# Rotary turn of queries and keys: the projection split in two parts from PSUM, each permuted by a product of its own

## Chip, cores and metric

The kernel runs on one core of a Trainium2 chip. The core has five engines with an instruction queue each: TensorE (PE), VectorE (DVE), ScalarE (ACT), GpSimd (POOL) and SyncE (SP), from whose queue the DMAs named here are issued. The metric is the device time in microseconds of one execution; smaller is better.

## What is computed

The reference is a two-layer trunk over 1024 latent tokens with a prefix of 256 context tokens, width 1024, in fp32. In each layer one input projection feeds three token mixers (windowed grouped-query attention, an SSD scan and a gated DeltaNet scan), whose outputs are joined and go through one output projection; a squared-ReLU MLP follows. Cut to what matters here, a two-dimensional rotary turn of the latent queries and keys ahead of the attention:

```python
def rot(u, pos):                      # u: 32 of the 64 columns of a head
    ang = pos[:, None] * inv_freq[None, :]
    u1, u2 = jnp.split(u, 2, axis=-1)
    return jnp.concatenate([u1 * cos - u2 * sin, u2 * cos + u1 * sin], axis=-1)

def window_gqa_attention(q_c, k_c, v_c, q_l, k_l, v_l, sink, need_ctx):
    q_l = rope_2d(q_l)                # rows turn the first half of a head, columns the second
    k_l = rope_2d(k_l)
    ...
```

Context tokens aren't turned.

## The kernel before

**Layout.** Activations lie with features on partitions and tokens on the free axis. The 1280 tokens (context first) are three chunks, `CHUNKS`: 256, 512 and 512 tokens; the first is the context. A block of 128 projected features is the product of eight 128x128 weight tiles with one chunk, accumulated in a PSUM bank `ps`. Precision is bought by splitting: every operand is a sum of a rounded fp32r part and its rest (`wh`, `wl` of weights, L192 and L193; `hl` of activations), and `proj` (L204) makes three products of each pair of tiles, 24 per block and chunk.

**The turn.** `rest()` (from L518) handles the blocks that aren't needed first; blocks 16 and 17 are the four query heads, 18 the two key heads (`j` = 0, 1, 2). Each of the three has two latent chunks, so there are 6 turns in a layer and 12 in the kernel. `perm` is a signed 128x128 permutation that brings u2 to u1's place with its sign and the reverse. For a latent chunk: SP loads the chunk of the table `rope` (cosines and sines, 512 KB) into a tile of tag `sil`, which has two buffers (L550); ACT copies `ps` to `rx` (L552); TensorE multiplies it with `perm` in fp32 into `rt` (L554); DVE makes `ry` = `rt` x sine (L556); POOL makes `rx` x cosine (L557) and adds `ry` (L558). The sum is split once more into `athl`: ACT casts (L560), DVE takes the rest (L561). `athl` is another tile of tag `sil`. From it SP stores four pieces for queries (L572) or six for keys (L567, L568) to scratch in DRAM (`attq`, `attk`), from where the attention loads them later. A context chunk skips the turn and is only split and stored. `rx` and `ry` share the two buffers of tag `st` with the copies of `to_tm` (L431).

**What sets the order.** The program is written as generators that are interleaved: while the last blocks of the projection run, the DeltaNet's inversion (`gQ`, `gT` products, DVE transposes L730, L735) and the first steps of its scan run too. A scan step has four groups of 12 small products, `vps`, `tps`, `sps` and `ops` (L837, L845, L856, L865), each waiting for a copy or a difference made from the one before; its inputs `stp`, `sv`, `sW` come by SP. Once the projection is done, attention (`asc`, `apT`, `aop`), SSD (from `sseg`, L891) and the rest of the scan run interleaved; each unit of the scan ends in `finish`: a norm (`osq`, `oss`, L800), a transposition `on` (L805), the gate `oz` (L806) and a store. The out-projection (`pu`, L204 again) follows. Within these bounds the compiler orders every engine's instructions by the program's priorities and a time line of its own, so an edit at one place may change the order of others further down.

Of the kernel before, what the change touches and what calls it, by code (L numbers as in the profile page):

```python
# [141 lines left out]
def kernel(ctx: ExitStack, tc: tile.TileContext, a: dict, out: bass.AP, dbg=None):  # L142
# [15 lines left out]
    with tc.tile_pool(name="cs0", bufs=1) as c0:  # L158
        cs2 = c0.tile([128, len(CN) - NF, 128], F32, name="cs2")
        nc.sync.dma_start(out=cs2, in_=csrc[:, NF:])  # L160
        for i, n in enumerate(CN[NF:]):
            d_, dt_ = (CR, F32R) if i < 3 else (CB, BF16)
            d_[n] = cp.tile([128, 128], dt_, name="c" + n)
            V.tensor_copy(out=d_[n], in_=cs2[:, i])
    pair = CR["pair"].bitcast(F32)
# [213 lines left out]
    def in_proj(l, hl, prm, R, es):  # L379
# [44 lines left out]
        def to_tm(s, dst, more=None):  # L424
            for u0 in (0, 4, 8):
# [4 lines left out]
                st = ip.tile([128, 4, 128], F32, tag="st", name="st")  # L430
# [87 lines left out]
        def rest():  # L518
# [24 lines left out]
            to_tm(s, lambda u0, n: R["attv"][:, u0:u0 + n])  # L543
            for j in range(3):
                for t0, n, ps in block(16 + j, ctxs=j == 2 or not last):
                    if t0 < LC:
                        x = ps[:, :n]
                    else:
                        rope = ip.tile([128, 2, 512], F32, tag="sil", name="rope", bufs=2)
                        nc.sync.dma_start(out=rope, in_=a["rope"][:, :, t0 - LC:t0 - LC + n])  # L550
                        x = ip.tile([128, 512], F32, tag="st", name="rx")
                        S.copy(out=x, in_=ps)  # L552
                        rt = Q["p"].tile([128, 512], F32, tag="pq", name="rt")
                        P.matmul(out=rt, lhsT=C["perm"], rhs=x, start=True, stop=True)  # L554
                        y = ip.tile([128, 512], F32, tag="st", name="ry")
                        V.tensor_tensor(out=y, in0=rt, in1=rope[:, 1], op=MULT)  # L556
                        G.tensor_tensor(out=x, in0=x, in1=rope[:, 0], op=MULT)  # L557
                        G.tensor_tensor(out=x, in0=x, in1=y, op=ADD)  # L558
                    t = ip.tile([128, 2, 512], F32R, tag="sil", name="athl", bufs=2)
                    S.copy(out=t[:, 0, :n], in_=x)  # L560
                    V.tensor_tensor(out=t[:, 1, :n], in0=x, in1=t[:, 0, :n].bitcast(F32), op=SUB)  # L561
                    t = t.bitcast(F32)
                    for g in range(2):
                        gs = slice(64 * g, 64 * g + 64)
                        if j == 2:
                            for g2 in range(2):
# [1202 lines left out]
```

## Time and profile before

| | us |
|---|---|
| time, median of 3 runs | 3470.7 (3467.23 to 3475.13) |
| the profiled execution, its own time | 3474.11 |
| span of that execution in the trace | 3472.3 |
| TensorE busy in it | 3169.3 |
| VectorE busy | 2367.8 |
| ScalarE busy | 1795.9 |
| GpSimd busy | 926.2 |
| mean granted TensorE clock | 0.956 of 2.4 GHz |

The span runs from the first to the last instruction. An engine's busy time leaves out its waits and its issue of DMAs; records of matmuls overlap at their ends, so the time of one product is better read from the distance between starts. In a timeline row the number in square brackets is the engine's idle time ahead of the row and what ended it. An fp32 product has two records in the trace, a product of fp32r or bf16 one; a group of 12 scan products, which are fp32, has 24.

### The profile page before, as it was taken

Reading aid. Unit: us, or ns where it says so; the run is one execution under the profiler, and the core shown is the slowest. Engines: PE = TensorE matmul, PEld = TensorE weight load, DVE = VectorE, ACT = ScalarE, POOL = GpSimd, SP = SyncE. Lnnn points to the kernel's source line nnn. Section 1 sums busy time; section 2 is a strip of 40 time slices with the busy share of each in tenths; the row PEclk is TensorE's granted clock in tenths of the full one; section 3 lists DMA queues with packets and bytes.
Section 4 is the critical chain, followed back from the end, with each engine's and each line's share of the span. In section 5 each row is a group of like instructions: output and inputs, shape, how many; then the busy total and the mean of one; then the engine's idle time right before and its main releaser. Section 6 shows DMA issues by size and latency. Waiting matters only on the chain. (4 is left out here: it accounts for less than half of the span.)

```text
span 3472.3 us, 56181 instructions
## 1 busy us (share of the span) xinstructions
PE 3169.3 (91%) x20912; PEld 2510.2 (72%) x20912; DVE 2367.8 (68%) x3725; ACT 1795.9 (52%) x3197; POOL 926.2 (27%) x822
## 2 busy tenths in 40 slices
PE   4998898899998999999989898798899998999998
PEld 1766787766676688788879666676677776887886
DVE  6568972178578556777785646986288487667776
ACT  4665533365556456444465556552366565555443
POOL 3228423477131000000120434723475120000001
PEclk8999899899999999999999999998899999999999
DMA  5467437765455754544445564745864455645442
GB/s 194 139 197 204 133 103 208 236 194 153 147 200 183 282 181 168 172 146 146 140 150 178 191 187 116 193 125 143 267 205 141 168 188 210 207 151 185 158 156 105
DMA packets 386743, 603.25 MB, mean 174 GB/s; under 512 B 64566, under 2 KB 195494, under 8 KB 382374
## 3 DMA queue, kind: packets, MB, share of 16 engines
q1 hardware_dynamic: 383590, 585.51, 53.0%
q0 software_dynamic: 2880, 14.16, 1.3%
q8 instruction: 164, 2.69, 0.3%
q14 instruction: 109, 0.89, 0.1%
HBM read 430.09 MB, written 169.46 MB: 173 GB/s over the span
## 5 line engine op out<-in xcount | busy, mean ns | idle before, releaser
L1414 PE MATMUL pu<-x,wh 128*128 128x512 f32 x3072 | 958.9, 395 | 32.4 <-ACT wh L192 14.8
L1414 PEld LDWEIGHTS pu<-x,wh 128*128 128x128 f32 x3072 | 581.0, 190 | 168.0 <-ACT wh L192 20.3
L204 PE MATMUL ps<-x,wh 128*128 128x512 f32 (+1 forms) x2288 | 681.5, 382 | 7.3 <-ACT ub L405 6.4
L1414 PE MATMUL pu<-x,wl 128*128 128x512 f32 x1536 | 597.5, 393 | 3.2 <-DVE wl L193 3.2
L204 PEld LDWEIGHTS ps<-x,wh 128*128 128x128 f32 x2288 | 420.5, 196 | 99.5 <-issue 21.6
L299 POOL TENSOR_TENSOR nacc<-nacc,nsq 128x512 f32<-128x512 f32 (+1 forms) x60 | 86.3, 1439 | 1520.8 <-ACT nsq L298 1323.4
L204 PE MATMUL ps<-x,wl 128*128 128x512 f32 (+1 forms) x1144 | 428.4, 377 | 3.5 <-POOL wl L193 3.5
L192 ACT CAST wh<-raw 128x512 fp32r<-128x512 f32 (+1 forms) x328 | 200.8, 615 | 275.3 <-PE ps L204 82.7
L1414 PEld LDWEIGHTS pu<-x,wl 128*128 128x128 f32 x1536 | 291.0, 189 | 67.2 <-DVE wl L193 5.7
L420 DVE SCALAR_TENSOR_TENSOR sil<-ub,cw,sil 128x256 f32<-128x256 f32 (+1 forms) x236 | 273.5, 1179 | 50.2 <-ACT sil L418 44.2
L204 PE MATMUL pu<-x,wh 128*128 128x256 f32 (+1 forms) x1152 | 284.7, 339 | 17.2 <-ACT x L1350 13.5
L193 POOL TENSOR_TENSOR wl<-raw,wh 128x512 fp32r<-128x512 f32 (+1 forms) x120 | 175.6, 1465 | 416.8 <-ACT wh L192 380.5
L193 DVE TENSOR_TENSOR wl<-raw,wh 128x512 fp32r<-128x512 f32 x208 | 156.1, 758 | 150.8 <-ACT wh L192 144.0
L204 PEld LDWEIGHTS ps<-x,wl 128*128 128x128 f32 x1144 | 222.6, 195 | 46.7 <-issue 7.0
L204 PEld LDWEIGHTS pu<-x,wh 128*128 128x128 f32 x1152 | 200.4, 195 | 44.1 <-issue 10.5
L204 PE MATMUL pu<-x,wl 128*128 128x256 f32 (+1 forms) x576 | 194.5, 339 | 14.1 <-DVE wl L193 14.0
L192 ACT CAST wh<-A 128x512 fp32r<-128x512 f32 x192 | 118.7, 619 | 139.5 <-PE pu L1414 133.7
L193 DVE TENSOR_TENSOR wl<-A,wh 128x512 fp32r<-128x512 f32 x192 | 135.7, 708 | 70.4 <-ACT wh L192 70.3
L1414 PE MATMUL pu<-xb,wh 128*128 128x512 f32 x512 | 163.9, 401 | 4.6 <-ACT h L1464 4.5
L1604 ACT CAST x<-x 128x1024 fp32r<-128x1024 f32 x112 | 111.9, 1048 | 103.8 <-DMA x<-th 97.9
L1662 DVE TENSOR_TENSOR xb<-pu,xb 128x512 f32<-128x512 f32 x192 | 131.1, 684 | 46.2 <-PE pu L1414 46.2
L192 ACT CAST wh<-S 128x512 fp32r<-128x512 f32 x128 | 79.0, 620 | 145.4 <-PE pu L1414 116.7
(354 smaller groups left out, 6133.1 us busy)
## 6 DMA issues: line engine op xcount, KB each, us to landing
x<-th SPq DMA_DIRECT2D x56, 1024.0 KB, 5.4
aw<-in_wada_dram SPq DMA_DIRECT2D x96, 512.0 KB, 5.7
A<-in_w_dram SPq DMA_DIRECT2D x164, 256.0 KB, 3.1
raw<-in_w_dram SPq DMA_DIRECT2D x128, 256.0 KB, 2.9
th<-h SPq DMA_DIRECT2D x128, 256.0 KB, 2.6
raw<-in_winf_dram SPq DMA_DIRECT2D x116, 256.0 KB, 3.5
stp<-rt SPq DMA_DIRECT2D x36, 768.0 KB, 5.3
xb<-in_w_dram SPq DMA_DIRECT2D x24, 1024.0 KB, 4.9
```

The source lines that it names most:

```text
L192: S.copy(out=wh[:, :n], in_=raw)
L193: eng.tensor_tensor(out=wl[:, :n], in0=raw, in1=wh[:, :n].bitcast(F32), op=SUB)
L204: P.matmul(out=ps[:, :n], lhsT=w_[:, k], rhs=x_[4 * g + k][:, :n], start=(g + k + j == 0), stop=(g == 1 and k == 3 and j == 2))
L299: eng.tensor_tensor(out=acc[:, :n], in0=acc[:, :n], in1=sq[:, :n], op=ADD)
L420: V.scalar_tensor_tensor(out=acc, in0=u[:, o + k:o + k + n], scalar=w[:, bi, k:k + 1], in1=acc, op0=MULT, op1=ADD)
L1414: P.matmul(out=ps, lhsT=w_[:, j], rhs=x_, start=first and j + i == 0, stop=(j == 3 and i == 2), skip_group_check=True)
L1604: S.copy(out=hi, in_=raw)
L1662: V.tensor_tensor(out=y[:, m], in0=ps, in1=y[:, m], op=ADD)
```

## The change

For a latent chunk ACT now casts `ps` to the rounded part `rxh`, and DVE takes the rest `rxl` = `ps` - `rxh`, both in fp32r; TensorE permutes each with `permr`, a rounded copy of `perm` made once, and sums the two products in `rt`. DVE multiplies `ps` with the cosines inside the table's tile, then `rt` with the sines in the tile's other half, and adds both there. The split of the sum (`put_att`) overwrites the same tile, and the stores read it. So a turn has one tile of tag `sil` in place of two; tag `st` has three buffers. GpSimd has no part in it. The second half of a turn (`rotate`) is written behind the next chunk's first half. Context chunks are split into a tile `athl` of their own as before.

```diff
+    permr = cp.tile([128, 128], F32R, name="permr")
+    V.tensor_copy(out=permr, in_=C["perm"])
...
-                st = ip.tile([128, 4, 128], F32, tag="st", name="st")
+                st = ip.tile([128, 4, 128], F32, tag="st", name="st", bufs=3)
...
+            def put_att(j, t0, n, x, t):
+                S.copy(out=t[:, 0, :n].bitcast(F32R), in_=x)
+                V.tensor_tensor(out=t[:, 1, :n], in0=x, in1=t[:, 0, :n], op=SUB)
...
+            def rotate(j, t0, n, rope, parts_):
+                rt = Q["p"].tile([128, 512], F32, tag="pq", name="rt")
+                for i, x in enumerate(parts_):
+                    P.matmul(out=rt, lhsT=permr, rhs=x, start=i == 0, stop=i == 1)
+                V.tensor_tensor(out=rope[:, 1], in0=rt, in1=rope[:, 1], op=MULT)
+                V.tensor_tensor(out=rope[:, 1], in0=rope[:, 0], in1=rope[:, 1], op=ADD)
+                put_att(j, t0, n, rope[:, 1], rope)
+
             for j in range(3):
+                turned = []
                 for t0, n, ps in block(16 + j, ctxs=j == 2 or not last):
                     if t0 < LC:
-                        x = ps[:, :n]
-                    else:
-                        rope = ip.tile([128, 2, 512], F32, tag="sil", name="rope", bufs=2)
-                        nc.sync.dma_start(out=rope, in_=a["rope"][:, :, t0 - LC:t0 - LC + n])
-                        x = ip.tile([128, 512], F32, tag="st", name="rx")
-                        S.copy(out=x, in_=ps)
-                        rt = Q["p"].tile([128, 512], F32, tag="pq", name="rt")
-                        P.matmul(out=rt, lhsT=C["perm"], rhs=x, start=True, stop=True)
-                        y = ip.tile([128, 512], F32, tag="st", name="ry")
-                        V.tensor_tensor(out=y, in0=rt, in1=rope[:, 1], op=MULT)
-                        G.tensor_tensor(out=x, in0=x, in1=rope[:, 0], op=MULT)
-                        G.tensor_tensor(out=x, in0=x, in1=y, op=ADD)
-                    t = ip.tile([128, 2, 512], F32R, tag="sil", name="athl", bufs=2)
-                    S.copy(out=t[:, 0, :n], in_=x)
-                    V.tensor_tensor(out=t[:, 1, :n], in0=x, in1=t[:, 0, :n].bitcast(F32), op=SUB)
...
+                        put_att(j, t0, n, ps[:, :n], ip.tile([128, 2, 512], F32, tag="sil", name="athl", bufs=2))
+                        continue
+                    rope = ip.tile([128, 2, 512], F32, tag="sil", name="rope", bufs=2)
+                    nc.sync.dma_start(out=rope, in_=a["rope"][:, :, t0 - LC:t0 - LC + n])
+                    xh = ip.tile([128, 512], F32R, tag="st", name="rxh", bufs=3)
+                    S.copy(out=xh, in_=ps)
+                    V.tensor_tensor(out=rope[:, 0], in0=ps, in1=rope[:, 0], op=MULT)
+                    if turned:
+                        rotate(*turned.pop())
+                    xl = ip.tile([128, 512], F32R, tag="st", name="rxl", bufs=3)
+                    V.tensor_tensor(out=xl, in0=ps, in1=xh.bitcast(F32), op=SUB)
+                    turned.append((j, t0, n, rope, (xh, xl)))
+                rotate(*turned.pop())
```

The line numbers of the new kernel are two larger up to `to_tm` and 14 larger behind the turn (L837 is L851 there). The instructions are the same on every engine up to the first `rt`, but for the copy to `permr`; behind it the order differs in the rest of the mixers of layer 0 and, from the input projection on, of layer 1. Three places follow.

VectorE, layer 0, the first two turns, before (`vd` belongs to the scan):

```order
L839 TENSOR_TENSOR vd<-vps,sv 128x384
L556 TENSOR_TENSOR ry<-rt,rope 128x512
L561 TENSOR_TENSOR athl<-rx,athl 128x512
L839 TENSOR_TENSOR vd<-vps,sv 128x384
L556 TENSOR_TENSOR ry<-rt,rope 128x512
L839 TENSOR_TENSOR vd<-vps,sv 128x384
L561 TENSOR_TENSOR athl<-rx,athl 128x512
```

The same place with the change:

```order
L853 TENSOR_TENSOR vd<-vps,sv 128x384 x2
L581 TENSOR_TENSOR rope<-ps,rope 128x512
L585 TENSOR_TENSOR rxl<-ps,rxh 128x512
L567 TENSOR_TENSOR rope<-rt,rope 128x512
L568 TENSOR_TENSOR rope<-rope 128x512
L581 TENSOR_TENSOR rope<-ps,rope 128x512
L585 TENSOR_TENSOR rxl<-ps,rxh 128x512
L549 TENSOR_TENSOR rope<-rope 128x512
L567 TENSOR_TENSOR rope<-rt,rope 128x512
```

The product of `ps` with the table (L581) stands ahead of the rest `rxl` (L585), which the second `rt` product reads; the first turn's split (L549) now stands behind the second turn's L581 and L585.

TensorE, layer 0, around the first `rt`, before (`ps` are products of the projection):

```order
L204 MATMUL ps<-x_437,wh 128x256
L204 MATMUL ps<-x_438,wh 128x256
L554 MATMUL rt<-rx,cst 128x512
L204 MATMUL ps<-x_437,wl 128x256
L204 MATMUL ps<-x,wh 128x512 x2
L204 MATMUL ps<-x,wl 128x512
```

The second product of the first turn, with the change (the first one stands 65 rows ahead; `vps`, `tps` belong to the scan):

```order
L851 MATMUL vps<-X_5717,stp 64x64
L859 MATMUL tps<-vd,stp 64x64 x12
L566 MATMUL rt<-rxl,permr 128x512
L206 MATMUL ps<-x,wh 128x512 x2
L206 MATMUL ps<-x,wl 128x512
```

Before, the product stood among the projection's products of one chunk, and the next chunk's came right behind; now six groups of the scan stand between the first and the second product, and the next chunk's products stand behind the second.

TensorE, the end of layer 1's mixers, before (`on` belongs to the scan's `finish`, `pu` to the out-projection):

```order
L1141 MATMUL apT<-cst,aP 128x128 x4
L805 MATMUL on<-cst,oacc 128x128 x3
L1141 MATMUL apT<-cst,aP 128x128 x4
L1147 MATMUL aop<-aPT,attv 64x256
L1141 MATMUL apT<-cst,aP 128x128 x4
L1147 MATMUL aop<-aPT,attv 64x256 x3
L1141 MATMUL apT<-cst,aP 128x128 x4
L1147 MATMUL aop<-aPT,attv 64x256 x4
L204 MATMUL pu<-x,wh 128x512 x3
```

With the change (`ops` is the last group of the scan):

```order
L879 MATMUL ops<-X_26284,stp 64x64
L1155 MATMUL apT<-cst,aP 128x128 x4
L1161 MATMUL aop<-aPT,attv 64x256 x3
L1155 MATMUL apT<-cst,aP 128x128 x4
L1161 MATMUL aop<-aPT,attv 64x256 x4
L819 MATMUL on<-cst,oacc 128x128 x6
L206 MATMUL pu<-x,wh 128x512 x3
```

The last scan group now stands ahead of the last eight `apT`, and the six `on` behind the last `aop`, right ahead of the out-projection.

## Rows read from the trace of the kernel before

**Rows 1.** The page, busy time of each engine, share of the span, instructions.

```profile
PE 3169.3 (91%) x20912; PEld 2510.2 (72%) x20912; DVE 2367.8 (68%) x3725; ACT 1795.9 (52%) x3197; POOL 926.2 (27%) x822
```

**Rows 2.** Busy us (count) by stretch: PE, PEld, DVE, ACT, POOL; granted clock, DMA share, GB/s.

```profile
528.60:660.85 132.25, 118.53 (x1218) 95.39 (x1217) 21.69 (x38) 43.47 (x88) 47.31 (x44) 0.99 0.70 212
2363.00:2481.80 118.80, 102.38 (x1131) 80.34 (x1129) 42.10 (x60) 34.95 (x63) 42.73 (x38) 0.89 0.62 183
```

**Rows 3.** TensorE's waits, 515 to 660 us: total us, times, longest.

```profile
PE rt L554 <- ACT rx L552: 10.0, 4, 4.2
```

**Rows 4.** TensorE's waits, 2365 to 2480 us.

```profile
PE rt L554 <- ACT rx L552: 9.3, 4, 5.0
```

**Rows 5.** ScalarE's timeline, layer 1: start, us, operation, idle time before, releaser.

```profile
2411.02 0.62 ACT L560 CAST athl<-rx 128x512 fp32r<-128x512 f32 x1 [8.80 <-POOL rx L558]
2411.66 0.58 ACT L552 COPY rx<-ps 128x512 f32<-128x512 f32 x1
```

**Rows 6.** TensorE's timeline, layer 1, the longest wait.

```profile
2412.30 2.07 PE L554 MATMUL rt<-rx,cst 128*128 128x512 f32 x2 [4.99 <-ACT rx L552]
2413.39 1.84 PE L204 MATMUL ps<-x,wh 128*128 128x512 f32 x2
...
2416.65 0.63 PE L204 MATMUL ps<-x,wh 128*128 128x512 f32 x2
```

**Rows 7.** VectorE's timeline, layer 0, the first table product.

```profile
550.38 0.69 DVE L556 TENSOR_TENSOR ry<-rt,rope 128x512 f32<-128x512 f32 x1 [7.55 <-DMA rope<-in_rope_dram]
```

**Rows 8.** TensorE's timeline, layer 0, around one `rt`.

```profile
546.10 0.91 PE L845 MATMUL tps<-vd,stp 64*64 64x64 f32 x24
...
554.38 1.13 PE L554 MATMUL rt<-rx,cst 128*128 128x512 f32 x2 [2.84 <-ACT rx L552]
554.94 1.03 PE L204 MATMUL ps<-x,wh 128*128 128x512 f32 x2
555.81 0.40 PE L204 MATMUL ps<-x,wl 128*128 128x512 f32 x1
556.04 0.62 PE L204 MATMUL ps<-x,wh 128*128 128x512 f32 x2
```

**Rows 9.** Views of `rope`, `rx` and `athl`: count, ns min/median/max; landing.

```profile
L556 DVE TENSOR_TENSOR ry<-rt,rope x12: 691/692/693, 550.4 to 2454.9; 128x512 f32<-128x512 f32 x12
DMA to landing us min/median/max: 3.8/4.1/4.4
...
L558 POOL TENSOR_TENSOR rx<-rx,ry x12: 1259/1264/1292, 551.8 to 2456.6; 128x512 f32<-128x512 f32 x12
L560 ACT CAST athl<-rx x12: 612/617/622, 553.1 to 2457.9; 128x512 fp32r<-128x512 f32 x12
L561 DVE TENSOR_TENSOR athl<-rx,athl x12: 691/692/1087, 553.7 to 2458.6; 128x512 fp32r<-128x512 f32 x12
...
DMA to landing us min/median/max: 2.1/3.1/6.3
```

**Rows 10.** VectorE's timeline, layer 0, one `oacc`.

```profile
591.52 1.65 DVE L800 TENSOR_TENSOR oacc<-oacc,oss 128x384 f32<-128x384 f32 x1 [0.36 <-POOL oss L799]
```

**Rows 11.** VectorE's timeline, layer 1, the inversion's transposes.

```profile
2375.78 4.06 DVE L730 STREAM_TRANSPOSE Lb<-XX 128x1024 f32<-128x1024 f32 x2
```

**Rows 12.** TensorE's timeline, the first `sseg` of either layer.

```profile
660.85 0.68 PE L891 MATMUL sseg<-ag,cst 128*128 128x60 f32 x4 [1.10 <-ACT wst L901]
...
2481.78 0.88 PE L891 MATMUL sseg<-ag,cst 128*128 128x60 f32 x6 [0.18 <-ACT zg L579]
```

**Rows 13.** Timelines of TensorE and VectorE, end of layer 1's mixers.

```profile
2685.38 0.74 PE L865 MATMUL ops<-X,stp 128*64 128x64 f32 x18
...
2696.51 0.66 PE L1141 MATMUL apT<-cst,aP 128*128 128x128 f32 x4
...
2707.39 1.65 PE L204 MATMUL pu<-x,wh 128*128 128x512 f32 x3 [6.83 <-ACT x L1350]
...
2695.15 0.62 DVE L806 SCALAR_TENSOR_TENSOR oz<-on,dg,oz 128x384 f32<-128x384 f32 x1 [0.70 <-PE on L805]
```

More of the change, by code (lines that the diff above doesn't have):

```diff
@@ L543, in rest @@
             to_tm(s, lambda u0, n: R["attv"][:, u0:u0 + n])
+            def put_att(j, t0, n, x, t):
+                S.copy(out=t[:, 0, :n].bitcast(F32R), in_=x)
+                V.tensor_tensor(out=t[:, 1, :n], in0=x, in1=t[:, 0, :n], op=SUB)
+                t = t.bitcast(F32)
+                for g in range(2):
+                    gs = slice(64 * g, 64 * g + 64)
+                    if j == 2:
+                        for g2 in range(2):
+                            nc.sync.dma_start(out=R["attk"][64 * g2:64 * g2 + 64, g, t0:t0 + n], in_=t[gs, 0, :n])
+                        nc.sync.dma_start(out=R["attk"][gs, 2, t0:t0 + n], in_=t[gs, 1, :n])
+                    else:
+                        for k in range(2):
+                            o = 64 * (g ^ k)
+                            nc.sync.dma_start(out=R["attq"][t0 // 128:(t0 + n) // 128, o:o + 64, 2 * g + j].rearrange("u p f -> p u f"),
+                                              in_=t[gs, k, :n].rearrange("p (u f) -> p u f", f=128))
@@ L559, in rest @@
-                    t = ip.tile([128, 2, 512], F32R, tag="sil", name="athl", bufs=2)
-                    S.copy(out=t[:, 0, :n], in_=x)
-                    V.tensor_tensor(out=t[:, 1, :n], in0=x, in1=t[:, 0, :n].bitcast(F32), op=SUB)
[L562 to L566, printed above, removed]
-                                nc.sync.dma_start(out=R["attk"][64 * g2:64 * g2 + 64, g, t0:t0 + n], in_=t[gs, 0, :n])
-                            nc.sync.dma_start(out=R["attk"][gs, 2, t0:t0 + n], in_=t[gs, 1, :n])
-                        else:
-                            for k in range(2):
-                                o = 64 * (g ^ k)
-                                nc.sync.dma_start(out=R["attq"][t0 // 128:(t0 + n) // 128, o:o + 64, 2 * g + j].rearrange("u p f -> p u f"),
-                                                  in_=t[gs, k, :n].rearrange("p (u f) -> p u f", f=128))
+                        put_att(j, t0, n, ps[:, :n], ip.tile([128, 2, 512], F32, tag="sil", name="athl", bufs=2))
```

## The prediction, made before the changed kernel was run

> **What bounds the kernel now.** I first read the page's line of busy times: TensorE is busy 91% of the span [rows 1], so a change of the time has to come out of TensorE's idle time, out of its products, or out of its clock. The rotation lies in two stretches, one per layer, from the last products ahead of the first `rt` to the first `sseg`, with which the attention, SSD and DeltaNet work begins. The view of busy time by stretch gives them 132.25 and 118.8 us, with TensorE busy 118.5 and 102.4 [rows 2]: 13.7 and 16.4 us are idle, and the second runs at a mean granted clock of 0.89. That is the whole store this change can draw on, beside its own products.
>
> Next the waits of TensorE in both stretches: `rt` of L554 waits for ACT's copy `rx` (L552) 10.0 us in layer 0 and 9.3 us in layer 1, four times in each [rows 3, 4]. All else there is small. Why the copy is late shows in ACT's timeline at the longest one: the cast `athl` of the chunk before stands idle 8.80 us for POOL's `rx` (L558), and the next chunk's copy runs only right behind it, at 2411.66 [rows 5]. The product follows at 2412.30, after 4.99 us of idle time [rows 6]. The pair of products behind it has a record of 1.84 us; a pair some 3 us later has 0.63 [rows 6], so the clock had dropped to the lower level, 1.2 GHz, and came back. And POOL is late because the table is late: VectorE's `ry` at 550.38 had idled 7.55 us for the `rope` load [rows 7]. So the table's arrival, then ACT's order, then TensorE.
>
> **What the change removes.** (1) Products. In the PE timeline `rt` starts at 554.38 and the `wl` product of the first triple at 555.81, with two `wh` products between; the next product starts 0.23 after that one [rows 8]. So the fp32 product takes 1.43 - 2 x 0.23 = 0.97 us. The change makes two fp32r products of it, which I price as the neighbours of the same shape and type: 0.46. That saves 0.51 x 12 = 6 us of TensorE, 3 in each layer, and all of it is on TensorE's path. The rows hold this exactly, so its bounds are narrow, 5 to 6.5.
> (2) The 10.0 + 9.3 us of waits for `rx`: POOL's two operations (some 1.26 us each [rows 9]) leave the chain, and ACT's cast of the next chunk no longer stands behind a cast that waits for POOL. Whether the time comes back depends on what is late next.
>
> **What it adds.** (3) VectorE. Two operations per chunk (L556, L561) become five of 128x512. Each is 0.69 us [rows 9], with the operand in PSUM (L556) or without (L561), so 3 x 0.69 x 12 = 25 us more on VectorE, and one copy of `perm` at the start (a 128x128 tile, far from any wait). VectorE is busy 68% [rows 1], and in these stretches 21.7 of 132 and 42.1 of 119 us [rows 2]: it has room, so I put this at 0, save where one of the five stands in a chain. The worst of the rows: `athl` once took 1.09 us against 0.69 [rows 9], so up to 60 x 0.4 = 24 us of VectorE more; it would be in idle time as well.
> VectorE's `oacc` of L800, both inputs in SBUF, took 1.65 us at 591.52 [rows 10], while POOL worked. The Trainium skill, "SBUF — State Buffer", section "Who interferes with whom", says that a VectorE instruction with two SBUF inputs and a GpSimd instruction that reads SBUF shut each other out for a whole instruction. By that rule the new sums (two SBUF inputs, one more per chunk than before) can each lose a GpSimd operation's time, and the removal of POOL's 24 operations gives back about as much; the trace agrees as far as this row goes, and the sum would be the same by either reading.
>
> (4) The wait that takes the old one's place. `rt` now needs `rxl`, and on VectorE the product with the table's cosine half, in place in the table tile, stands in the row ahead of `rxl` (it is so in the order shown). So TensorE's second product waits for the table, where before the product waited only for the copy of the chunk before. And the tile holds table, sum and result in one: the load for chunk n+2 may start only when the output DMAs of chunk n have landed. Before, the table's tile was free after VectorE and POOL had read it. The loop of one tile, from rows [rows 9]: table landing 4.1, five VectorE operations 3.5, ACT's cast 0.6, the product 0.2, four DMA issues of some 0.6 and the last one's landing 3.1: 13.9 us, for two chunks, if nothing is in the way. TensorE has 2 x 24 in-projection products of 0.23, 11 us, per such pair and several groups of the DeltaNet scan; the loop also has VectorE's, ACT's and SP's other work in it.
> I went through the new order by hand with the durations of before. Layer 0: the first table load has the same place on SP's queue, so it lands at 550.4 as before [rows 7]; cosine product and `rxl` 1.4 more, hence `rt` at 552. Between the two `rt` products stand only 14 products of half the width, 0.12 each by that, and six groups of the scan of 0.91 at most (24 records, as at 546.10 [rows 8]): some 7 us of work and the scan's own waits, from 538.4 on, where before 24 products of the next chunk stood there as well. So TensorE would idle 3.6 to 5.8 us there. The third and fifth chunk (same tile again) come at 575 and 597.5 with some 2.9 and 3.8 us; the others without. Sum 10.3 to 12.5, in place of 10.0. In layer 1 the same way: 2.1 behind the transposes of the inversion that stand on VectorE (the first pair took 4.06 us [rows 11]), 0.4, 5.9 for the fourth chunk's table, 2.5 and 1.2: 12.1 in place of 9.3; the other waits there (`gQ`, scan) become about 5.5 in place of 6.9. Bounds of this term: nothing (VectorE's order lets `rxl` pass, the waits vanish) and 19 (each as long as the longest today, 4.99, four times in either layer).
> (5) The longest waits bring half a clock with them. At the level of rows 6 this is some 1 to 2 us in layer 0 (the fifth is then shorter) and nothing sure in layer 1, where 5.9 takes the place of 4.99.
> (6) The number of DMAs stays, the same loads and 76 outputs, only issued from another tile. The third buffer of tag `st` (L431 too) I put at 0: no wait for one is among those of TensorE there [rows 3, 4]; the bound is a gain of some 1 us. What is queued behind a waiting `rope` load on SP, in program order, is weight loads (`raw`) and the loads of the scan (`sv`, `sW`, `stp`). The in-projection's weights are some chunks ahead; the scan isn't.
> (7) Order downstream. By the hand replay `sseg` of layer 0 comes some 5 to 10 us before 660.85 [rows 12], but with 30 of the scan's groups done and not 33 (2.6 us to be done later); in layer 1 some 7 to 9 us before 2481.78 [rows 12], with five groups less (4.3 us). TensorE-bound as the next stage is, that work comes back in full. So the two stretches give: layer 0, 3 + 10.0 - 11.4 + 1.5, about 3 by waits, and 2 to 7 by positions, I take 5; layer 1, 3 + 9.3 - 12.1 + 1.4, about 2 by waits and 4 by positions, I take 4. Together -9.
> (8) The end of layer 1's mixers. The last rows of TensorE before the out-projection are now the six `on` of the DeltaNet's last unit, behind the last `aop`. Before, `on` stood some 15 rows ahead. From the last `ops` product (2685.38 + 0.74) to the end of the last `oz` (2695.15 + 0.62) the chain took 9.65 us [rows 13]. In the new order the last `ops` have eight `apT` and seven `aop` behind them; that same lot ran from 2696.51 to 2700.56, where the 6.83 us of idle time ahead of 2707.39 begin [rows 13], so 4.05 us. The last `oz` would then be done 9.65 - 4.05 = 5.6 us behind the last `aop`, and the out-projection starts so much later: I take +5, bounds 0 (the first products need other units) and +6. Layer 0's end keeps its order.
>
> **The sum.** -5 - 4 + 5 = -4 us: the profiled execution's 3474.11 would become 3470. That execution lies 3.4 over the median of the runs, so 3466.7, which I give as 3466.5. What a measurement of this kernel can tell from no change is about 0.2%, 6.9 us: faster begins below 3463.8 and slower above 3477.6.
>
> **Rivals.**
> A. The waits vanish. If VectorE's cosine product is never late, or the scan fills TensorE, then -19.3 (all waits for `rx`), -6 (products) and +5 (end): -20, 3450.5. For it: VectorE has idle time, and ACT's order no longer ties chunk to chunk. Against it: the table's load was the late one already [rows 7], and its tile now comes free later. 0.2.
> B. The waits move as I said, but layer 1's end costs nothing, since the scheduler's `on` may be ready long before (the scan's chain of before had slack), or the out-projection starts with other units: -9 to -10, 3461. 0.18.
> C. Slower: the table's return loop. Outputs landed within 3.1 us at the median and 6.3 at most [rows 9]. If behind a fuller SP queue each of the six pairs waits 2 us or more beyond my replay, for a landing that is nearer 6.3 or for an issue behind scan loads, TensorE waits 12 us more: 3466.5 + 12 = 3478.5, up to +19 with the full 3.2 each. It decides from 11 / 6 = 1.9 us per pair. For it: two tiles only, and results in them; against it: SP is seldom full in these stretches, and outputs of 0.1 MB each are short. 0.22.
> D. The change doesn't do what it says: for the second and fourth chunk of layer 0 the two products stand in neighbouring rows, so nothing of the next chunk is between them and the cast; that is in my replay already and gives no time of its own.
>
> **Chances.** Forecast (within 0.2%) 0.4; A 0.2 and B 0.18, faster; C 0.22, slower. So faster 0.38, same 0.4, slower 0.22. The range reaches to A's time on the one side and past C's nearer price on the other: 3449 to 3481. The forecast's own range, by the bounds of (7) and (8), is 3460 to 3473.
>
> **What would show it right or wrong.** The `rt` products in the profile after: half the TensorE time, 0.23 each (1). POOL without rows in the rotation (2). TensorE's waits for `rxl`, some five to eight of 1 to 6 us, with VectorE idle for the `rope` load ahead of them; if TensorE's waits before `rt` sum to under 5 us, A is right, and over 30, C (4). `sseg` at 649 to 656 and at 2465 to 2475 less what layer 0 gave (7). The out-projection of layer 1 starting 10 us or more behind the last `aop` (8). Wrong altogether would be a difference that lies outside these stages, in MLP or modulation, whose order on TensorE is the same row by row.

## The result and the profile after

The changed kernel takes 3507.7 us (median of four, 3504.6 to 3511.6) beside 3469.1 us before in the same comparison: 1.0099 of the time before, interval 1.0080 to 1.0118, so about 1% slower (39 us between the medians, 34 by the ratio). A second measurement (run e13) gave 3498.0 us and 1.0090, interval 1.0074 to 1.0107. The forecast was 3466.5, and the range to 3481 doesn't hold it.

The page's line of busy times, to be held against [rows 1]:

```profile
PE 3179.2 (91%) x20912; PEld 2519.2 (72%) x20912; DVE 2409.6 (69%) x3762; ACT 1800.4 (51%) x3199; POOL 893.5 (25%) x798
```

GpSimd lost 33 us, as the removal of its operations says; VectorE gained 42; TensorE's busy time rose by 10, though its products became cheaper. Four stretches show where the 34 us between the two spans (3506.3 and 3472.3) went: in each layer from the first `rt` to the first `sseg`, which I call the rotation's stage, and from there to the first product of the out-projection, the mixers' stage. Busy time by stretch, first of the changed kernel, then of the kernel before (columns as in [rows 2]):

```profile
532.90:651.40 118.50, 104.04 (x1085) 85.64 (x1083) 29.56 (x50) 35.88 (x72) 24.89 (x25) 0.96 0.70 207
651.40:919.00 267.60, 230.88 (x2218) 163.93 (x2218) 177.26 (x406) 145.14 (x342) 158.46 (x174) 0.87 0.53 166
2391.30:2491.90 100.60, 82.82 (x949) 65.02 (x947) 45.44 (x68) 29.12 (x51) 21.38 (x20) 0.92 0.64 182
2491.90:2738.90 247.00, 211.86 (x2493) 154.45 (x2493) 165.66 (x353) 139.98 (x318) 145.77 (x162) 0.90 0.62 191
```

```profile
538.40:658.60 120.20, 107.58 (x1156) 85.84 (x1154) 19.30 (x32) 38.55 (x77) 42.17 (x39) 0.99 0.69 210
658.60:904.40 245.80, 218.54 (x2146) 157.38 (x2146) 167.50 (x406) 142.44 (x336) 159.07 (x172) 0.91 0.57 177
2375.80:2481.80 106.00, 89.58 (x1070) 69.81 (x1068) 30.06 (x38) 31.77 (x57) 39.76 (x36) 0.87 0.66 193
2481.80:2707.40 225.60, 201.25 (x2374) 145.52 (x2374) 157.09 (x352) 136.67 (x312) 141.32 (x158) 0.95 0.63 192
```

The rotation's stages are 1.7 and 5.4 us shorter; ahead of the first `rt` another 5.5 us went. The mixers' stages are 21.8 and 21.4 us longer. What lies between and behind them changed by 0.9 and 2.5. So -5.5 - 1.7 + 21.8 + 0.9 - 5.4 + 21.4 + 2.5 = 34.0: the loss lies wholly behind the rotation, in work that the change doesn't touch.

Two cautions. The 5.5 us aren't a gain of the change: the instructions there are the same but for the copy to `permr`, and runs e10 and e12, whose order is the same up to there, reach their first `rt` at 538.2 and 530.1. So one trace of each kernel splits the loss no finer than some 8 us a stretch. And the rotation's stages hold less work: by TensorE's counts three and five scan groups (72 and 119 records) have moved from them into the mixers' stages. By the prediction's estimate these are 2.6 and 4.3 us, about the 7.1 us by which the rotation's stages are shorter, so the rotation itself shows no gain here.

In the rotation's stages the waits ahead of `rt`, to be held against [rows 3, 4], are now of VectorE's `rxl`, in the changed kernel's list of TensorE's waits (us, times, longest; layer 0, then layer 1):

```profile
PE rt L566 <- DVE rxl L585: 11.9, 3, 5.2
...
PE rt L566 <- DVE rxl L585: 9.1, 4, 3.3
PE rt L566 <- DVE rope L567: 1.2, 1, 1.2
```

Layer 0's 11.9 us are in place of 10.0, layer 1's 10.3 in place of 9.3. The first of them, on VectorE and TensorE:

```profile
545.44 0.69 DVE L581 TENSOR_TENSOR rope<-ps,rope 128x512 f32<-128x512 f32 x1 [3.78 <-DMA rope<-in_rope_dram]
546.04 0.68 DVE L585 TENSOR_TENSOR rxl<-ps,rxh 128x512 fp32r<-128x512 f32 x1
...
546.78 0.79 PE L566 MATMUL rt<-rxl,permr 128*128 128x512 f32 x1 [4.16 <-DVE rxl L585]
```

VectorE stood idle for the table; the cosine product L581 went first, `rxl` (L585) behind it, and TensorE had waited 4.16 us for that. A product of either part passes in 0.23 us where the clock is full, as here in layer 1 (the starts of the rows):

```profile
2402.16 0.40 PE L566 MATMUL rt<-rxh,permr 128*128 128x512 f32 x1
2402.40 0.40 PE L206 MATMUL ps<-x,wl 128*128 128x512 f32 x1
2402.63 0.39 PE L566 MATMUL rt<-rxl,permr 128*128 128x512 f32 x1
2402.86 0.40 PE L206 MATMUL ps<-x,wh 128*128 128x256 f32 x2
```

The end of layer 1's mixers on TensorE, VectorE and ScalarE, against [rows 13]:

```profile
2720.50 1.08 PE L1161 MATMUL aop<-aPT,attv 128*64 128x256 f32 x6 [0.16 <-ACT aPT L1156]
2723.84 0.79 PE L819 MATMUL on<-cst,oacc 128*128 128x128 f32 x3 [2.27 <-DVE oacc L814]
2725.47 0.90 PE L819 MATMUL on<-cst,oacc 128*128 128x128 f32 x3 [0.84 <-DVE oz L820]
2726.41 0.62 DVE L820 SCALAR_TENSOR_TENSOR oz<-on,dg,oz 128x384 f32<-128x384 f32 x1 [1.00 <-PE on L819]
...
2738.25 2.18 ACT L1364 CAST x<-xb 128x512 fp32r<-128x512 f32 x4 [15.22 <-DMA xb<-rm]
2738.92 1.65 PE L206 MATMUL pu<-x,wh 128*128 128x512 f32 x3 [12.54 <-ACT x L1364]
```

The last `aop` is followed by two waits of `on` (2.27 and 0.84 us), and the out-projection then waits 12.54 us where it waited 6.83. From the end of the last `aop` (2721.58) to the out-projection it is 17.3 us, 10.5 more than the 6.8 of before. The last `oz` ends 5.4 us behind that `aop`, and 11.9 us more pass until its store is read back as `x` (`xb`, then ScalarE's cast).

What the mixers' stage of layer 0 lost shows in its stretches: busy time and clock of the changed kernel from 686 to 760, then of the kernel before from the start of its stage to 760.

```profile
686.00:694.00 8.00, 2.86 (x72) 2.45 (x72) 6.82 (x13) 4.96 (x11) 6.43 (x8) 0.94 0.73 228
694.00:703.00 9.00, 8.98 (x46) 6.67 (x46) 3.20 (x9) 4.26 (x11) 5.88 (x6) 0.50 0.37 122
703.00:729.00 26.00, 24.84 (x295) 18.52 (x294) 19.40 (x46) 14.33 (x36) 20.39 (x22) 1.00 0.67 214
729.00:732.00 3.00, 1.03 (x25) 0.89 (x26) 3.00 (x8) 1.54 (x4) 0.60 (x1) 0.76 0.48 110
732.00:748.00 16.00, 15.98 (x124) 10.79 (x125) 6.56 (x17) 8.90 (x20) 8.73 (x11) 0.51 0.50 165
748.00:760.00 12.00, 12.00 (x108) 8.92 (x108) 9.10 (x19) 7.93 (x16) 8.37 (x9) 1.00 0.34 91
```

```profile
658.60:700.00 41.40, 35.15 (x331) 28.31 (x333) 15.47 (x42) 16.11 (x44) 24.64 (x26) 0.67 0.75 254
700.00:760.00 60.00, 57.69 (x639) 41.20 (x636) 45.58 (x110) 41.38 (x94) 48.48 (x54) 1.00 0.67 209
```

From 694 to 703 and from 732 to 748 the granted clock is 0.50, the lower of its two levels, and between them 1.00. What came ahead of each fall, in TensorE's timeline of the changed kernel:

```profile
694.01 0.48 PE L1155 MATMUL apT<-cst,aP 128*128 128x128 f32 x1 [4.04 <-ACT aP L1138]
...
729.03 0.92 PE L859 MATMUL tps<-vd,stp 64*64 64x64 f32 x24 [1.20 <-DVE vd L853]
731.88 0.47 PE L879 MATMUL ops<-X,stp 128*64 128x64 f32 x2 [1.94 <-ACT X L861]
```

A wait of 4.04 us for the softmax on ScalarE, and two of 1.20 and 1.94 us for links of the scan's chain. In the kernel before the 60 us up to 760 ran at full clock, but the 41 ahead of them only at 0.67: the low clock isn't new, there is more of it. Counting (1 - clock) x length as lost, the mixers' stages lose 34.8 and 24.7 us so, before 22.1 and 11.3: 13 us more in each. Some of that falls on waits, where it costs nothing.

The rows of the mixers' stages above split what was lost without counting anything twice. In layer 0 TensorE was busy 12.3 us longer and idle 9.5 longer (36.7 against 27.3), in layer 1 busy 10.6 and idle 10.8 longer (35.1 against 24.3). Of the busy time 2.6 and 4.3 us are the moved scan groups; the other 9.7 and 6.3 are the same products taking longer, and for those only the clock is in sight. The idle time is waits in the new order; 8.8 us of layer 1's are at its end (5.7 more ahead of the out-projection, 3.1 of `on`).

### The profile page after: what moved, and what is told of

Same layout as the page of the kernel before. It is cut to its first block, busy times and chain, and to the rows that moved or that the text cites. A ratio compares the mean times of both kernels' runs of the same rounds, so it can differ in the third digit from the quotient of the medians.

```text
span 3506.3 us, 56140 instructions
## 1 busy us (share of the span) xinstructions
PE 3179.2 (91%) x20912; PEld 2519.2 (72%) x20912; DVE 2409.6 (69%) x3762; ACT 1800.4 (51%) x3199; POOL 893.5 (25%) x798
```

## The experiments

Two theories: **O**, the compiler's new order of the mixers' stage costs the time, and the rotation by itself doesn't; **R**, the rotation as it is now written (the table's tile held up to the stores, five operations on VectorE, queries and keys stored later) costs it, wherever it stands. One table for all; the four stage times are of one profiled execution each, the time and its ratio to the kernel before (with interval) of several. The stage "rotation 1" doesn't hold the same work in all of them: TensorE has 949 records in it in the changed kernel, 637 in e4, 661 in e5.

| run | what | time, us | ratio (interval) | rotation 0 | mixers 0 | rotation 1 | mixers 1 |
|---|---|---|---|---|---|---|---|
| before | | 3469 to 3473 | 1 | 120.2 | 245.8 | 106.0 | 225.6 |
| after | | 3507.7 | 1.0099 (1.0080 to 1.0118) | 118.5 | 267.6 | 100.6 | 247.0 |
| e1 | before, plain order | 3856.2 | 1.1107 (1.1067 to 1.1147) | 186.8 | 258.6 | 159.7 | 207.8 |
| e2 | after, plain order | 3811.2 | 1.0977 (1.0933 to 1.1020) | 174.1 | 253.9 | 151.7 | 214.0 |
| e3 | before, third buffer | 3477.3 | 1.0023 (1.0002 to 1.0045) | 121.4 | 253.6 | 96.0 | 241.9 |
| e4 | after, `rxl` first | 3480.4 | 1.0028 (1.0005 to 1.0051) | 110.4 | 257.4 | 93.4 | 229.4 |
| e5 | after, table 1 | 3493.7 | 1.0056 (1.0039 to 1.0074) | 117.8 | 261.1 | 97.7 | 227.6 |
| e6 | after, table 4 | 3469.6 | 0.9994 (0.9980 to 1.0009) | 119.0 | 248.1 | 95.1 | 230.2 |
| e7 | after, not deferred | 3494.6 | 1.0062 (1.0040 to 1.0084) | 117.4 | 265.4 | 101.7 | 250.4 |
| e8 | before, VectorE for GpSimd | 3476.4 | 1.0015 (0.9997 to 1.0032) | 114.3 | 269.5 | 98.2 | 239.3 |
| e9 | after, table 5 | 3461.5 | 0.9968 (0.9953 to 0.9983) | 115.0 | 256.9 | 97.8 | 226.8 |
| e10 | e4, table 4 | 3479.2 | 1.0028 (1.0009 to 1.0046) | 111.4 | 263.8 | 93.2 | 231.9 |
| e11 | before, table 4 | 3480.9 | 1.0019 (0.9999 to 1.0039) | 119.7 | 248.0 | 105.5 | 240.1 |
| e12 | e4, table 5 | 3479.6 | 1.0029 (1.0008 to 1.0051) | 109.0 | 257.4 | 93.0 | 239.1 |
| e13 | after again | 3498.0 | 1.0090 (1.0074 to 1.0107) | 117.1 | 264.9 | 103.1 | 250.0 |
| e14 | after, table 6 | 3467.0 | 0.9998 (0.9979 to 1.0016) | 118.4 | 250.4 | 97.3 | 228.5 |
| e15 | after, two buffers | 3496.7 | 1.0082 (1.0062 to 1.0101) | 115.0 | 267.0 | 112.7 | 234.6 |

**e1 and e2: the rotation under one and the same later order.** Both kernels with the compiler's time line off:

```diff
-    with tile.TileContext(nc, schedule_with_timeline_sim=True) as tc:
+    with tile.TileContext(nc, schedule_with_timeline_sim=False) as tc:
```

> The kernel before with the compiler's own time line switched off: every engine keeps program priority, and the order of the stage behind the projection (attention, SSD, rest of the scan) is then the same, row by row, with either rotation. It is the base for the next run; its own time is expected well above 3470 us in either theory, since the order of before rests on the time line. Theory O (order): the 38 us lie in the new order of the stage behind the rotation, not in the rotation. Theory R (rotation): the new rotation itself costs them, wherever it stands.

> The changed kernel with the time line switched off, to be held against the run before it, whose later order is the same row by row. Theory O: the rotation by itself gains what its products save and some waits, so 3 to 15 us faster than that run. Theory R: 20 to 40 us slower than it.

Measured: 3856.2 and 3811.2, so the changed kernel is 45 us **faster**. R expected 20 to 40 slower and falls; O's sign holds, its size (3 to 15) doesn't. About 21 of the 45 us lie in the rotation's stages (12.7 and 8.0), 26 ahead of the first `rt` of either layer (687.1 to 670.2, and 1603.0 to 1594.3 from the out-projection to the next `rt`), where of the change only the third buffer stands; the mixers' stages change by -4.7 and +6.2. The split is of one trace each, so part of it can be scatter; the 45 us are between medians of four. TensorE's waits ahead of `rt` in e2 are next to nothing, 0.4 and 1.7 us. The cover is another one here, since without the time line the scan runs ahead of the rotation, so this bounds no size for the tuned order.

**e3, e8, e15: parts of the change alone, or without one.** e3, the old rotation with the third buffer:

```diff
-                st = ip.tile([128, 4, 128], F32, tag="st", name="st")
+                st = ip.tile([128, 4, 128], F32, tag="st", name="st", bufs=3)
...
-                        x = ip.tile([128, 512], F32, tag="st", name="rx")
+                        x = ip.tile([128, 512], F32, tag="st", name="rx", bufs=3)
...
-                        y = ip.tile([128, 512], F32, tag="st", name="ry")
+                        y = ip.tile([128, 512], F32, tag="st", name="ry", bufs=3)
```

> The kernel before, rotation untouched, with three buffers of tag st in place of two; the compiler's order of the mixers behind it comes out as different from before's as the changed kernel's does. Theory O: the stage from the first sseg to the out-projection (245.8 us in layer 0 and 225.6 in layer 1 before) moves by more than 5 us in at least one layer, most likely longer, so the time is 3478 to 3510. Theory R: with the old rotation both stages stay within 5 us and the time within 3463 to 3478.

Measured 3477.3. One more buffer, with the old rotation, makes the mixers' stages 7.8 and 16.3 us longer, which R didn't allow, though the 7.8 alone could be scatter (one order scatters by up to 9, see e6 and e9 below); the stages ahead of them give most of it back (layer 1's rotation 10.0 shorter), and the time rose by 0.2%, a little under O's 3478 and inside R's 3463 to 3478. So a new order doesn't have to cost 1%, and a longer mixers' stage is in part work moved over from the stage ahead.

e8, the old rotation with GpSimd's two operations on VectorE:

```diff
-                        G.tensor_tensor(out=x, in0=x, in1=rope[:, 0], op=MULT)
-                        G.tensor_tensor(out=x, in0=x, in1=y, op=ADD)
+                        V.tensor_tensor(out=x, in0=x, in1=rope[:, 0], op=MULT)
+                        V.tensor_tensor(out=x, in0=x, in1=y, op=ADD)
```

> The kernel before with the rotation's two GpSimd operations on VectorE, nothing else: the part of the change that takes GpSimd out, alone. Both put the waits for rx at less than 19.3 us (VectorE needs 0.69 us for each, not 1.26). Theory O: the later order is new again (its likeness to before's is as low as the changed kernel's), the stages behind take 245 to 270 and 225 to 250 us, time 3465 to 3505. Theory R, if it is VectorE's added work that costs: 3490 to 3510; if not, 3455 to 3470.

Measured 3476.4, ratio 1.0015: taking GpSimd out costs nothing that can be told. The waits for `rx` fell from 19.3 to 15.0 us. The mixers' stage of layer 0 took 269.5 us, as long as the changed kernel's, with the old rotation; the stages ahead of the mixers' are 5.9 and 7.8 us shorter, and from layer 0's out-projection to the next `rt` it was 1460.1 us, not 1471.4. So a long mixers' stage in one trace isn't yet a slow kernel, and the time has to be looked at beside it.

e15, the changed kernel with two buffers of tag `st`:

```diff
-                st = ip.tile([128, 4, 128], F32, tag="st", name="st", bufs=3)
+                st = ip.tile([128, 4, 128], F32, tag="st", name="st", bufs=2)
...
-                    xh = ip.tile([128, 512], F32R, tag="st", name="rxh", bufs=3)
+                    xh = ip.tile([128, 512], F32R, tag="st", name="rxh", bufs=2)
...
-                    xl = ip.tile([128, 512], F32R, tag="st", name="rxl", bufs=3)
+                    xl = ip.tile([128, 512], F32R, tag="st", name="rxl", bufs=2)
```

> The changed kernel with two buffers of tag st as before. Theory O: rotation of layer 0 within 4 us of 118.5, later order new in layer 1, time 3470 to 3512. Theory R with the third buffer as the cause: under 3475, and the waits ahead of rt gone.

Measured 3496.7: the third buffer isn't the cause. In layer 0's mixers' stage the order came out the same as the changed kernel's on every engine, and it took 267.0 us.

**e5, e6, e7, e13, e14: the rotation kept, the later order changed.** The table `SPANS` says from where to where in the mixers' stage each of the three streams (scan, SSD, attention) is interleaved, a row for each layer. Run e5 (table 1; the later tables show the new line alone):

```diff
-SPANS = (((-0.321, 0.75), (0, 0.95), (0, 1.05)), ((-0.458, 0.85), (-0.05, 1.05), (0, 1.0)))
+SPANS = (((-0.321, 0.7), (0, 0.95), (0, 1.05)), ((-0.458, 0.8), (-0.05, 1.05), (0, 1.0)))
```

> The changed kernel with two numbers of SPANS changed, the table that says how the scan, SSD and attention are interleaved behind the projection (the scan's end 0.75 to 0.70 in layer 0, 0.85 to 0.80 in layer 1). TensorE's order in layer 0 is row by row the changed kernel's up to the middle of the stage behind the rotation. Theory O (the loss is in the order of that stage): rotation stage of layer 0 within 2 us of 118.5, the stage behind it off 267.6 by more than 4 us; in layer 1 the last on stands ahead of the last aop again, so the wait ahead of the out-projection is back from 12.5 to about 7; time 3470 to 3500. Theory R (the rotation and what it delays cost it): the stage behind stays within 4 us of 267.6 and the time at 3500 to 3512.

Run e6 (table 4):

```diff
+SPANS = (((-0.321, 0.75), (0, 1.0), (0, 1.0)), ((-0.458, 0.75), (-0.05, 1.0), (0, 1.0)))
```

> The changed kernel with other numbers of the same table (SSD and attention end at 1.0 in both layers, the scan of layer 1 at 0.75); TensorE's order of layer 0 is the changed kernel's up to a little behind the first sseg. Theory O: the stage behind the rotation of layer 0 differs from 267.6 by more than 4 us, either way; in layer 1 the last on still stands behind the last aop, so the wait ahead of its out-projection stays 11 to 13 us; time 3480 to 3515. Theory R: 267.6 within 4 us, time 3500 to 3512.

Run e7, each turn finished at once:

```diff
-                    if turned:
-                        rotate(*turned.pop())
...
-                    turned.append((j, t0, n, rope, (xh, xl)))
-                rotate(*turned.pop())
+                    rotate(j, t0, n, rope, (xh, xl))
```

> The changed kernel with each turn finished at once, not behind the next chunk's first half. TensorE's order of layer 0 is the same row by row, so both theories expect 118.5 and 267.6 us there again, within 3 (if these move by more, neither holds, and it is the chip that scatters). Layer 1's order differs from the end of the rotation on: theory O expects its stage behind (247.0) to differ by more than 4 us, theory R within 4; time 3490 to 3515.

In layer 0 the rotation's stage is the changed kernel's in all three, and its times repeat (117.8, 119.0, 117.4). The mixers' stage behind it took 261.1, 248.1 and, with the changed kernel's own order, 265.4. In e5 the wait ahead of layer 1's out-projection is back at 6.91 us, as expected. e6 has the kernel before's time, with the new rotation in full, and so is better than O's 3480 to 3515, which I had set too high. In layer 1 of e7 the order differs from the end of the rotation on, but its mixers' stage kept its length (250.4 against 247.0), where O had expected another. Busy time of the mixers' stage of layer 0 in e6:

```profile
652.60:900.70 248.10, 217.36 (x2218) 155.05 (x2218) 172.65 (x406) 145.03 (x342) 158.00 (x174) 0.94 0.58 179
```

TensorE has 2218 records in it as in the changed kernel, hence the same work, but a mean clock of 0.94 and not 0.87, and 13.5 us less busy time.

Runs e6 and e9 have one and the same order of layer 0's mixers on every engine and gave 248.1 and 256.9, so I measured how much of it is scatter: the changed kernel again (e13, no edit), and beside it e14 (table 6), which takes only layer 0's numbers from e6:

```diff
+SPANS = (((-0.321, 0.75), (0, 1.0), (0, 1.0)), ((-0.458, 0.85), (-0.05, 1.05), (0, 1.0)))
```

> The changed kernel once more, on the chip of the next two runs. If its order sets the stage behind the rotation of layer 0: again 260 to 272 us (267.6, and 265.4 in run e7 with the same order), time 3495 to 3512. If that was scatter: 248 to 260, time 3470 to 3490.

> The changed kernel with only the two numbers of layer 0 of run e6 (SSD and attention end at 1.0), layer 1's numbers as they are. If order sets it: the stage behind the rotation of layer 0 at 245 to 258 (248.1 and 256.9 in e6 and e9, same order), at least 5 us under the run before; the last on of layer 1 stands ahead of the last aop, wait ahead of the out-projection about 7; time 3455 to 3470. If scatter: both runs within 5 us of each other there.

The mixers' stage of layer 0, in e13 and then in e14:

```profile
651.30:916.20 264.90, 228.18 (x2218) 161.87 (x2218) 178.54 (x406) 145.05 (x342) 158.48 (x174) 0.89 0.54 167
```

```profile
651.30:901.70 250.40, 221.94 (x2217) 157.71 (x2217) 173.46 (x405) 145.50 (x342) 160.13 (x174) 0.91 0.58 177
```

The changed kernel's order gave 267.6, 265.4 (e7), 264.9 and, in e15, 267.0; e6's order 248.1, 256.9 and 250.4, with the same rotation and the same work (2217 or 2218 records on TensorE in all seven). Their means are 266.2 and 251.8: 14 us by the order alone, where one order scatters by up to 9. Of the 14, 9 are TensorE's busy time (means 230.9 and 221.8) and 5 its idle time. In e14 the last `on` stands ahead of the last `aop`, and the wait ahead of layer 1's out-projection is 8.44 us, where 7 was expected:

```profile
2691.38 0.55 PE L819 MATMUL on<-cst,oacc 128*128 128x128 f32 x3
2691.85 1.08 PE L1161 MATMUL aop<-aPT,attv 128*64 128x256 f32 x6
2701.37 1.65 PE L206 MATMUL pu<-x,wh 128*128 128x512 f32 x3 [8.44 <-ACT x L1364]
```

In e6 it was still 12.77, and e6's layer 1 was no slower on the whole: from one out-projection to the next it took 1800.5 us, e14 1799.7, the kernel before 1803.0, the changed kernel 1819.9 and in e13 1818.1. So the late `on` is there, but it isn't what decides layer 1.

**e4, e10, e12: the wait for the table moved off `rt`.** `rxl` is written ahead of the cosine product:

```diff
-                    V.tensor_tensor(out=rope[:, 0], in0=ps, in1=rope[:, 0], op=MULT)
-                    if turned:
-                        rotate(*turned.pop())
                     xl = ip.tile([128, 512], F32R, tag="st", name="rxl", bufs=3)
                     V.tensor_tensor(out=xl, in0=ps, in1=xh.bitcast(F32), op=SUB)
+                    V.tensor_tensor(out=rope[:, 0], in0=ps, in1=rope[:, 0], op=MULT)
+                    if turned:
+                        rotate(*turned.pop())
```

> The changed kernel with rxl written ahead of the product of ps with the table, so TensorE's second product no longer waits for the table; the later order comes out different once more. Theory O: the rotation's waits fall (21 us of waits for rxl to under 12), but the time is set by how the later stage falls out, anywhere from 3470 to 3515, and the stage behind differs from 267.6 and 247 us by more than 5 us in a layer. Theory R: the later stage keeps its 267 and 247 us within 5, the time is 3495 to 3505.

Measured 3480.4: by the ratios some 25 us of the loss are gone, but not all. No wait ahead of `rt` is left; the projection's products wait for the cosine product instead, which holds the PSUM bank (layer 0, then layer 1):

```profile
PE ps L206 <- DVE rope L583: 5.7, 3, 2.8
...
PE ps L206 <- DVE rope L583: 12.4, 2, 7.8
```

So the wait is halved in layer 0 (11.9 before the edit) and longer in layer 1 (10.3): together 18.1 us, where O expected under 12. The rotation's stages are 8.1 and 7.2 us shorter than the changed kernel's, but hold less work, so these aren't the price of the wait. With the two tables of e6 and e9:

> Run e4 (rxl ahead of the product with the table) with the table of run e6. Theory O: the rotation stages keep e4's times (110 and 93 us within 4), no wait for rxl, the stages behind take what their new order gives, 240 to 260 and 220 to 240; time 3445 to 3485, the middle of it below the kernel before. Theory R: 3480 to 3505.

> Run e4 with the table of run e9: layer 0's order is that of run e10, layer 1's differs. Theory O: layer 0's two stages repeat e10's within 3 us each, layer 1's stage behind differs from e10's by more than 3; time 3445 to 3485. Theory R: 3480 to 3505.

Measured 3479.2 and 3479.6. The rotation's stages repeat e4's, and the mixers' stages take 263.8 and 231.9, 257.4 and 239.1: a table that helps one order doesn't help another. Layer 0's order is the same in these two and still gave 263.8 and 257.4, so the 3 us expected were too narrow.

**e11 and e9: the table with the old rotation, and the best version.** The kernel before with the table of e6:

> The kernel before with the table of run e6, rotation untouched: how much of e6 is the table and how much the rotation. Theory O: its stages behind the rotation move too, by up to 15 us in a layer, either way (245.8 and 225.6 before); the table was fitted to before's arrival times, so more likely slower: 3465 to 3490. Theory R: within 4 us of them, 3465 to 3475.

Measured 3480.9, 1.0019 (0.9999 to 1.0039). The same table that takes the whole 1% off the changed kernel takes nothing off the old one. Table 5, e6's row for layer 0 with 0.80 for the scan's end in layer 1:

```diff
+SPANS = (((-0.321, 0.75), (0, 1.0), (0, 1.0)), ((-0.458, 0.8), (-0.05, 1.05), (0, 1.0)))
```

> The changed kernel with the table's numbers of run e6 for layer 0 (SSD and attention end at 1.0) and, for layer 1, the changed kernel's own but the scan's end at 0.80. Layer 0's order on TensorE is that of e6, in layer 1 the last on stands four rows ahead of the out-projection, before the last aop. Theory O: layer 0 repeats 119 and 248 us within 3, the wait ahead of layer 1's out-projection falls from 12.8 to 7 to 9 and the waits of on vanish, so 3460 to 3470. Theory R: 3490 to 3512.

Measured 3461.5, ratio 0.9968 (0.9953 to 0.9983): 0.3% faster than the kernel before and, by the two ratios, 1.3% faster than the changed one. Layer 0 took 115.0 and 256.9 us, not e6's 119 and 248 within 3. e14, which differs from it only in that 0.80, has 0.9998 (0.9979 to 1.0016), so the safe statement is that the new rotation with a refitted table isn't slower than the kernel before, and was once faster by 0.3%.

## Why the prediction was wrong, point by point

- **Products (1)**: right. 0.23 us for each part's product.
- **The old waits (2)**: right that they go, and that GpSimd leaves the chain.
- **VectorE (3)**: right at nothing on the path. Its busy time rose by 42 us; the new operations are 26 of them, as forecast (25), the rest is other operations that took longer.
- **The new wait (4)**: right in place, cause and size. Forecast were 10.3 to 12.5 and 12.1 us, with 3.6 to 5.8 for the first; measured are 11.9, 10.3 and 4.16, though the first table landed at 545.4 and not at 550.4. The upper bound of 19 beside it doesn't come out of its own sum: eight waits of 4.99 are 40, and the forecast of 22 to 25 lies above 19. What the waits cost isn't shown, since e4 moved them and didn't remove them.
- **Positions (7), first half**: right in layer 0 by luck. The first `sseg` came 7.2 us earlier (5 to 10), but 5.5 of it stand ahead of the first `rt`, where two executions of one order differ by 8; the stage itself gave 1.7, with 2.6 of work less in it, where I had counted 5. In layer 1 `sseg` came at 2491.9, which is 10.1 later, with 15.5 lost ahead of it: the stage gave 5.4 for the 4 counted, with 4.3 of work less.
- **Positions (7), second half: the step that failed.** "TensorE-bound as the next stage is, that work comes back in full" took the mixers' stage as a fixed amount of work, 2.6 and 4.3 us more by the moved scan groups. It became 21.8 and 21.4 us longer. I had seen that its whole order was new and counted that at nothing, with no rival for it; the sum and the range's upper end both lacked that term. By the runs it is worth some 14 us in layer 0 with the rotation unchanged (e6, e9, e14 against after, e7, e13, e15), and about 19 from one out-projection to the next in layer 1 (e6, e14 against after, e13).
- **The end of layer 1 (8)**: right in sign, half in size. The last `oz` ended 5.4 us behind the last `aop`, forecast 5.6. But the term let the out-projection follow `oz` as soon as it had followed `aop` (6.8 us), and that took 11.9, so it started 10.5 us later behind the last `aop`, over the bound of +6. Run e6 with a late `on` and a wait of 12.77 isn't slow, so the 10.5 may not be added to the rest.
- **Rival C**, the table's return loop, was the only slower one, and is wrong: the waits ahead of `rt` sum to 22 us, not over 30. A is wrong by the same number (under 5 was its mark), and B's saving at the end of layer 1 didn't come.

Shown: the loss isn't in the rotation, and the same rotation under another order of the mixers' stage loses none of it. What is argued and not shown alone: how much of it the clock carries. The same products took 9.7 and 6.3 us longer than before, and 9 of the 14 us between the two orders of layer 0 are busy time; but the clock, the waits and the order always moved together, and no run held one of them still. Open too is which of the new neighbours in the order matter, and why layer 1's stage stayed at 250 in e7 while its order changed.

## What to carry to other kernels

Where a compiler's time line orders the instructions, an edit's price has two parts: what it does at its place, and what the new order does to every stage behind it. Here the first was a few us, and the second 43 us over two stages (7 of them work moved there) with one table and nothing that can be told in the time with another; a forecast needs a term and a range for it as soon as the order behind the edit isn't the same row by row. A change that wins locally should be judged only with the interleaving table refitted, or with the later order held the same: the 1% lost here was the old table under a new order.

## What the runs showed of the hardware

What a wait costs TensorE isn't told by its length alone. In the changed kernel it ran 9 us at the lower clock after a wait of 4.04 us, and 16 us after two of 1.20 and 1.94 us within 3 us. In the kernel before a wait of 3.02 us (ended at 676.74) was followed by 20 us at 0.50, one of 3.81 us (ended at 777.87) by 4 us at a mean of 0.57 and then full clock:

```profile
676.00:696.00 20.00, 18.55 (x125) 14.06 (x126) 7.26 (x24) 8.56 (x24) 12.24 (x12) 0.50 0.63 215
778.00:782.00 4.00, 4.00 (x54) 3.28 (x55) 1.75 (x4) 0.08 (x1) 0.00 (x0) 0.57 0.20 42
```

Between 700 and 760, with no wait over 0.73 us, it stayed at full clock. And one order of all engines isn't one time: the same stage took 248.1, 250.4 and 256.9 us in three executions, at mean clocks of 0.94, 0.91 and 0.89.
